# Two-layer encoder trunk on one core: gate, up and output projections in groups of six products, and a new order

## The chip, the core and the metric

The kernel runs on one core of a Trainium2 chip. The engines named below are TensorE (PE, matrix products; its weight loads are listed as PEld), VectorE (DVE), ScalarE (ACT), GpSimd (POOL) and SyncE (SP, which here issues the DMA transfers of the weights). The metric is the device time of one execution in microseconds (us), as the median of several runs; lower is better.

## The reference

The program computes two layers on one sequence of 256 rows of width 1024, all in float32. Cut to what matters here:

```python
def swiglu(x, w_gate, w_up, w_down):
    return (jax.nn.silu(x @ w_gate) * (x @ w_up)) @ w_down

def reference(x, mem, ...):
    mem_kv = mem @ w_mem_kv
    mem_k = split_heads(mem_kv[..., :MEM_WIDTH])
    mem_v = split_heads(mem_kv[..., MEM_WIDTH:])
    for i in range(DEPTH):                       # 2 layers
        x = layer_norm(ALPHA * x + 0.5 * swiglu(x, ffn1_w_gate[i], ffn1_w_up[i], ffn1_w_down[i]), ...)
        if i % N_MIXERS == 0:
            proj = x @ rwkv_w_in[j]              # 1024 -> 2560 + 256
            mix = rwkv7_mix(proj[..., :RWKV_SHIFT], ...)
        else:
            proj = x @ sb_w_in[j]                # 1024 -> 3*768 + 256
            mix = stick_breaking_mix(proj[..., :c], proj[..., c:2 * c], proj[..., 2 * c:3 * c])
        heads = jnp.concatenate([mix, memory_attention(mq, mem_k, mem_v)], axis=-1)
        x = layer_norm(ALPHA * x + heads @ w_out[i], ...)
        x = layer_norm(ALPHA * x + 0.5 * swiglu(x, ffn2_w_gate[i], ffn2_w_up[i], ffn2_w_down[i]), ...)
    return x
```

`rwkv7_mix` carries a 64 x 64 state for each of 12 heads along the 256 rows. `w_gate` and `w_up` are 1024 x 2816, `w_down` is 2816 x 1024. Most of the work is products of `x` with weights that are read once from memory.

## The kernel before

**Products in two parts.** PE multiplies a reduced float32 type (F32R) faster than float32, so most products are made of three. `piece()` loads 128 x 1024 weights into a raw buffer by DMA, ACT copies them to F32R (the high part, `hi`), and DVE subtracts that from the raw weights (the low part, `lo`). The rows of `x` are transposed on PE and split in the same way into `xTh` and `xTl`. `mm3` then adds, in one PSUM bank, xTh·hi, xTh·lo and xTl·hi. There are 11 raw, 9 high and 8 low buffers, which is why the same names (hi_7r, lo_8r) come again and again. In a matmul row of the profile `ps_29r<-hi_7r,xTh` reads: into bank ps_29r, hi_7r streams through (512 columns), and xTh is the stationary operand, 128 x 128.

**Tiles and stages.** The rows are two halves of 128. A feed-forward block (`ffn_block`) takes 256 columns of gate and of up: four pieces, each holding two of the eight 128-row steps k for 256 gate and 256 up columns. For each half 8 x 3 products go to a gate/up bank (ps_29r or ps_30r), then ACT and DVE make silu(gate)·up, PE transposes it, and `down` multiplies it into two accumulating banks of the half (ps_25r and ps_26r, ps_27r and ps_3r). For some blocks the down products are plain float32 ones, such as `ps_26r<-raw_51r,hT_945r`. Projections into the mixers and the output projection go through `cols_mm`, eight k with one `mm3` each. The transposes use banks ps_5r and ps_6r, which the mixers' small products use as well.

**What sets the order.** The code above doesn't issue anything: a planner (`Plan`) notes each operation with what it waits for, and a list scheduler then orders PE, DVE, ACT and the DMA queue of SP together, by a priority for each operation. The priorities stand in `URGENCY`, a packed table with one number for each operation in the order of the code. What `together()` encloses is one operation to the planner, an `mm3` for instance. The whole program is then issued in that order from one line in `Plan.issue` (L788 here, L785 in the changed kernel), so all rows of the profile show the same line, and groups are told apart by the names of the tiles.

**Stages in time.** From the start to 264 us the feed-forward blocks of the first layer run, then the mixer of the first half of the rows, whose state chain runs from 264 to 285 us. The state chain of the second half runs from 400 to 432 us. In such a chain products of the state (names with S_113r), additions on DVE, copies on ACT and products with L_345r follow each other for each chunk of 64 rows, and feed-forward products and projections fill PE between them. From 432 us on the feed-forward blocks of layer one and the whole of layer two follow, whose mixer has no such chain.

Of the kernel before, what the change touches and what calls it, by code (L numbers as in the profile page):

```python
# [18 lines left out]
AF = mybir.ActivationFunctionType  # L19
# [4 lines left out]
P = 128  # L24
D = 1024
KT = D // P
# [3 lines left out]
C = 64  # L30
# [7 lines left out]
FC = 256  # L38
# [34 lines left out]
FLAGS = dict(t1=False, bt=False, dc=False, out1=False, zl2=False, pb=False, xt=False, mn=False, tn=False, vn=False, sq=True)  # L73
# [45 lines left out]
class Engine_:  # L119
# [19 lines left out]
    'c-l?edAN<`8#exXZJ`Vel1617LVQJ~5}C>rqRb-7EK`I`Wr$LSMCK;Slp#|pG*IS>qJdB(A{9}r`}cX?{X35L{bL_{ueF}%zOVbb&g(qSYpq4?jW'  # L139
    'PDf62iEPL-_e@jPIvHSo{C~{J($qcFn#JLh3|}ef)hUX9#8d9-k4y$_p{h^!Sv=2mgw3_^}wryJv5%%-7$#D1<A#cI@}e=R02(LTk^hKJ|YexAJ('  # L140
    '!ADNH4U!M7Ru6rij9>V^`F-|xd<Fp1Lj6D)#hXXM_lr@Bh{VcG4`-?Jvf0NtwKg77r8kc4dp`|k|@N=KXH;A!a-VmBS6~d$r{>~S|oA&)j+%N8pv'
    '2TG8YJVH!(>FWh!59nrIb9)ye|N>$rd$Xmt^M)t7|WFop{cmCxc-49neiUa7DA14F>XGW`8b!yd;W{Dte9@I+{>QZw<v_JBSYx9C>=Ky3*q@ELMZ'
    'xFjJvCZutUD;&h+|(7{7G3`}V|m>D3`DbJj9qc=_WPH{KdT!8~&4JZI$bdgr-PEzbWE<42uBSo3#`n^wk{z9NKS_N*7x#C2a^A41JCav`>5kB9Jk'
    '+ZY#j58=v>V*I{r2%is%@tbQy7@-!goQW}iC9yi^DCd8%d<fS%%T3nVF2)sp3RDlFlCxc2G=z(<3L$ri5OVg7@f~qiliM4fjxn29N)-wr|H&A0T6'
    'e`maxIS!Hwodn4QjbQ#z&tCVaAuP^ZZn2*f%+ZLXXDy+vpIAf2Iz8w@~+D;;1Nw=-RPzxaF-F8~+sJyy+nfNQw8|7!URg;W0T~>8uxOsntX3Cy%+'
    'lk8y;!a@BF})9_R}#yQW&c%+8&zYXhm!%poG%J+zIbgvLPu2=f)F~0Cvj9+~i<6o^pxLfUOIM4TEVyq^A1=RA3>q59r9_wA33I!I*iSxX4PYA^d+'
    'wbmFsO{cdex8G+*{5SXaf@DZO`!+Hup-7iax?FS5WdV2W6|9q{AKN1+J}(6jI-FIhd#J5BO?@8k~`e>>YwrM3aPNOcskBcrT<SK6nid&()wc4Jux'
    'ml7Q)}lVti21n>B|MxNqc4kHX8579lLZS^n#VFkNj6sl`s`IaAHKPNd^2rBmVXzj8iMzF@lL+8B4~rTZI(Q2ogeIt+{PX8<mx*1y~z<LhnU4^FRX'
    'DZcz6xGc1mkN<v)u|%5~v&iuSS=2mxD*UQncER@eIWbO3$5_krH%<wm@_f1d2WA(9(0>TLT5}8>9~uzCp*Lb2G&qET{oNz>#baaKB7dtEIm2IK7#'
    '`zn*Z*)+jO*rwaI@!MUn3s5p3)rN9<g^<^{%d7W98nujel0#M!0C2{#CO9^1fBR#;t{!zti#D+i(Z7<3EqF^cx|dfcS&6uDw1LhMZ5w?)v>hn6Kb'  # L150
    '$-S?;COn90zTTN%B!tEE*@mGCx6Py-Q-%?+OFcGfmi=&FT#<UKhOScfF>Vt7JV;m`;ch?MIkep?mV$W;TXj2Fe&VtGPF}{qS3c~YfoHSgWs=g-wZ'
    '^7Ro_u_=Yui{>Lx+QBWZ2u!2d+Mvn_<NP}UDFQ+#6L;Sc2y1GQ#F6OMU3l<!@70vJC%-CKB}h9-&;R*EdhJhDsTV7xbS6!aqK(seGtM-N%&;4T09'
    'oQ{K_FL?4n0&$JnBGD&$`i;|#qr?|n7;i8lO|j`v(CrVsSXeXcDSLR<B?AcpdAGZQCGfd8w+T0^h2uN%Vme$Ny0P3~>|JFKZu3D<1KJ0Gjx2bZVg'
    'A9}OGarin8BOR^PEQE5MV;nNqHH}lDuo{-b7ro&ji#{DQFdh5;7D5v>p3y%Q=H3-!Q*q^8mX6zZ(WZ7G%!2O{a<TIzJmlV_*SpY^=k(meUfT&zv-'
    ';sPI=Esr9MFemU#Vxy5T2?Z!dcj@lkmR&>@mZ>8F&j%O~ogm61zLsr}}aVT)q7b{N)H?Bd+|g2_C+HSMlU1{Cz@gf2TS3;MF}-L%4jN`oewDYhr9'
    'Gwtg^QOOM<RFB|uzW1~G8Ve|*-SXYnFnPgwQw@IJg>h-E>)T>pDZ^`42@X=^pjQ{*Egs*Y)KxZu@)^_T(N*&(&I>!G-dAuitcm7Mq9l28B**v&Q4'
    '^&pGtn{bTelbr>$BcL6`{NMqxWrnkLwL7wI<8o(xBf>9^!A>LFh`Hp*|WQTObwUwg7S-tf02_s;wubOEk^Jat7v^T{joX5;>&R;JpU<<ulm3vt^b'
    '*3w<-xEH|d{RF^-XwT&rkIkq}PPuKn-DxWQ|CXw52|T8Iw4qNh&E?>2o=QS6r_7}C4V9uV*07)$#5o-bnTrj~nQex|%1_IEM$UaF?^)b>{W*HUfD'
# [633 lines left out]
def kernel(ctx, tc, const, x, mem, f1g, f1u, f1d, f2g, f2u, f2d, ln_g, ln_b, w_out, w_mem_kv,  # L792
                      rw_in, r_mu, r_w0, r_wup, r_a0, r_aup, r_gup, r_kk, r_ka, r_rk, r_lng, r_lnb, sb_in, out):
    nc = Plan(tc.nc)
# [206 lines left out]
    def ffn_block(w, c, halves, beside, whole):  # L1001
# [57 lines left out]
        hs = {}  # L1059
# [867 lines left out]
```

## Time and profile before

| | |
|---|---|
| Runs, median of 3 | 1056.89 us (1056.53 to 1056.94) |
| Profiled execution, own time | 1058.2 us |
| Its span in the profile | 1056.4 us, mean granted PE clock 0.995 |
| PE busy, PE weight loads busy | 99%, 79% of the span |
| DVE, ACT, POOL busy | 84%, 70%, 0% |
| DMA | 303.19 MB, 286 GB/s from and to HBM over the span |

The span is what the profiler recorded from the first to the last instruction; the own time of that execution has 1.8 us more around it, and is 1.3 us above the median of the runs. A busy share is an average over stages with different limits, so what counts is where PE waits. In the lists of groups and in the timelines the text in brackets, or after the last bar, is the idle time just before the instruction on its engine, and the engine and tile that ended it.

### The profile page before, as it was taken

What the parts mean: (1) busy time and instruction counts of PE and PEld (TensorE: products, weight loads), DVE (VectorE), ACT (ScalarE), POOL (GpSimd) and SP (SyncE); (2) the same over time, 40 slices, a digit from 0 to 9 for tenths busy, and PEclk for the clock granted to TensorE, in tenths of its full rate; (3) what the DMA queues carried; (4) which work ended last, traced back from release to release, by engine and by line L of the source; (5) the groups of instructions that cost most, each with busy time, mean ns of one, the idle gap of its engine ahead of it and who ended that gap; (6) DMA issues with size and microseconds to landing.
All of it is one profiled execution on the core that took longest, in us unless ns stands there. A gap on an engine that the chain in (4) does not pass through costs nothing.

```text
span 1056.4 us, 17846 instructions
## 1 busy us (share of the span) xinstructions
PE 1041.8 (99%) x6275; PEld 835.8 (79%) x6275; DVE 886.2 (84%) x1241; ACT 741.6 (70%) x1064; POOL 5.3 (0%) x20
## 2 busy tenths in 40 slices
PE   8999999999899999999999999999999999999997
PEld 7788888877788776688888888888778777888885
DVE  6776679999799998898799765569899999976688
ACT  6665558968679877667577555457987998765573
POOL 0000000000000000000000000000000000000000
PEclk9999999999899999999999999999999999999999
DMA  9998869879399788799999976768989989998792
GB/s 307 332 368 259 265 201 357 266 247 331 130 328 336 250 273 295 247 341 315 307 325 352 311 246 208 226 213 262 369 309 315 366 274 304 366 366 256 265 317 76
DMA packets 212684, 303.19 MB, mean 287 GB/s; under 512 B 13892, under 2 KB 159728, under 8 KB 212594
## 3 DMA queue, kind: packets, MB, share of 16 engines
q1 hardware_dynamic: 212050, 301.53, 85.2%
q8 instruction: 49, 0.80, 0.3%
q10 hardware_dynamic: 544, 0.52, 0.2%
q14 instruction: 41, 0.34, 0.1%
HBM read 300.95 MB, written 1.05 MB: 286 GB/s over the span
## 4 chain that ended last, share of the span: by engine, by line
PE 95%; DMA 2%; DVE 1%; ACT 1%; issue 0%; SPq 0%; DVEq 0%; ACTq 0%
PE ps_30r L788 28%; PE ps_29r L788 27%; PE ps_26r L788 8%; PE ps_3r L788 8%; PE ps_27r L788 8%; PE ps_25r L788 8%; PE ps_5r L788 3%; PE ps_6r L788 3%; DMA raw_9r<-in_ffn_w_down_dram 1%; DMA raw_18r<-in_ffn_w_up_dram 1%; DMA raw_48r<-in_ffn_w_up_dram 1%; DMA raw_12r<-in_ffn_w_up_dram 1%; DVE x L788 0%; DVE L_345r L788 0%; DVE lo_47r L788 0%
## 5 line engine op out<-in xcount | busy, mean ns | idle before, releaser
L788 PE MATMUL ps_30r<-hi_46r,xTh 128*128 128x512 f32 (+1 forms) x70 | 28.2, 403 | 0.0
L788 PE MATMUL ps_30r<-hi_46r,xTl 128*128 128x512 f32 (+1 forms) x70 | 26.9, 385 | 0.0
L788 PE MATMUL ps_30r<-lo_17r,xTh 128*128 128x512 f32 x68 | 26.5, 390 | 0.0
L788 PE MATMUL ps_29r<-lo_11r,xTh 128*128 128x512 f32 (+1 forms) x64 | 24.6, 385 | 0.8 <-DVE lo_11r L788 0.8
L788 PE MATMUL ps_30r<-lo_11r,xTh 128*128 128x512 f32 x64 | 25.0, 390 | 0.0
L788 PE MATMUL ps_30r<-hi_10r,xTh 128*128 128x512 f32 x60 | 24.5, 409 | 0.0
L788 PE MATMUL ps_30r<-lo_8r,xTh 128*128 128x512 f32 x62 | 24.2, 391 | 0.0
L788 PE MATMUL ps_30r<-hi_10r,xTl 128*128 128x512 f32 x60 | 23.5, 392 | 0.0
L788 PE MATMUL ps_30r<-lo_14r,xTh 128*128 128x512 f32 x60 | 23.4, 390 | 0.0
L788 PE MATMUL ps_29r<-hi_65r,xTh 128*128 128x512 f32 x56 | 22.8, 407 | 0.0
L788 PE MATMUL ps_29r<-lo_17r,xTh 128*128 128x512 f32 x58 | 22.6, 390 | 0.0
L788 PE MATMUL ps_29r<-lo_47r,xTh 128*128 128x512 f32 (+1 forms) x58 | 22.2, 383 | 0.0
L788 ACT ACTIVATE idle_2r<-ps_29r 128x256 f32<-128x256 f32 (+1 forms) x27 | 11.1, 412 | 15.8 <-PE ps_29r L788 15.2
L788 PE MATMUL ps_30r<-hi_7r,xTh 128*128 128x512 f32 (+1 forms) x56 | 21.9, 392 | 0.0
L788 PE MATMUL ps_29r<-hi_65r,xTl 128*128 128x512 f32 x56 | 21.9, 392 | 0.0
L788 ACT ACT_TABLE_LOAD x16 | 20.5, 1283 | 2.0 <-issue 1.7
L788 PE MATMUL ps_30r<-lo_41r,xTh 128*128 128x512 f32 x56 | 21.9, 390 | 0.0
L788 PE MATMUL ps_29r<-lo_14r,xTh 128*128 128x512 f32 x56 | 21.8, 390 | 0.0
L788 ACT ACTIVATE idle_1r<-ps_29r 128x256 f32<-128x256 f32 (+1 forms) x27 | 11.7, 432 | 14.3 <-PE ps_29r L788 14.3
L788 PE MATMUL ps_30r<-hi_7r,xTl 128*128 128x512 f32 (+1 forms) x56 | 21.4, 383 | 0.0
L788 PE MATMUL ps_30r<-hi_65r,xTh 128*128 128x512 f32 x52 | 21.4, 412 | 0.0
L788 ACT ACTIVATE idle_2r<-ps_30r 128x256 f32<-128x256 f32 (+1 forms) x30 | 12.9, 431 | 12.0 <-PE ps_30r L788 12.0
(2124 smaller groups left out, 3945.5 us busy)
## 6 DMA issues: line engine op xcount, KB each, us to landing
raw_9r<-in_ffn_w_down_dram SPq DMA_DIRECT2D x16, 512.0 KB, 6.7
raw_48r<-in_ffn_w_down_dram SPq DMA_DIRECT2D x16, 512.0 KB, 6.0
raw_12r<-in_ffn_w_down_dram SPq DMA_DIRECT2D x16, 512.0 KB, 6.2
raw_18r<-in_ffn_w_gate_dram SPq DMA_DIRECT2D x31, 256.0 KB, 5.0
raw_18r<-in_ffn_w_up_dram SPq DMA_DIRECT2D x31, 256.0 KB, 4.6
raw_15r<-in_ffn_w_down_dram SPq DMA_DIRECT2D x15, 512.0 KB, 5.8
raw_9r<-in_ffn_w_gate_dram SPq DMA_DIRECT2D x30, 256.0 KB, 5.9
raw_9r<-in_ffn_w_up_dram SPq DMA_DIRECT2D x30, 256.0 KB, 5.8
```

What stands on the lines that cost most here:

```text
L788: fn(*[at(x) for x in a], **{n: at(x) for n, x in k.items()})
```

## The change

In all gate and up products and in all projections through `cols_mm`, the eight steps k are taken in pairs. For the two k of a pair, `mm6` first makes the four products with the high part (xTh·hi and xTl·hi of the first k, then of the second), as one operation to the planner, and then the two products with the low part (xTh·lo of each), as a second operation. Before, each k had its own `mm3`: high, low, high. The products are the same, 5261 matmuls of the same shapes and operands; 944 triples become 472 groups of six. The down products and the products of the memory tokens keep `mm3`. Since two operations replace two, the table `URGENCY` keeps its length, and all its values are new, so that the order of the whole program is another one.

```diff
-FLAGS = dict(t1=False, bt=False, dc=False, out1=False, zl2=False, pb=False, xt=False, mn=False, tn=False, vn=False, sq=True)
+FLAGS = dict(t1=False, bt=False, dc=False, out1=False, zl2=False, pb=False, xt=False, mn=False, tn=False, vn=False, sq=True, lw=True)
...
 URGENCY = (
...
 )
...
+    def mm6(o, rows, start, stop):
+        with nc.together():
+            for i, (sh, sl, wh, wl) in enumerate(rows):
+                nc.tensor.matmul(o, sh, wh, start=start and i == 0, stop=False)
+                nc.tensor.matmul(o, sl, wh, start=False, stop=False)
+        with nc.together():
+            for i, (sh, sl, wh, wl) in enumerate(rows):
+                nc.tensor.matmul(o, sh, wl, start=False, stop=stop and i == len(rows) - 1)
+
     def cols_mm(o, xT, pieces):
+        if FLAGS["lw"]:
+            for i in range(0, KT, 2):
+                mm6(o, [(xT[0][:, k], xT[1][:, k], h, l) for k, h, l in pieces[i:i + 2]], i == 0, i == KT - 2)
+                yield
+                yield
+            return
         for i, (k, h, l) in enumerate(pieces):
             mm3(o, xT[0][:, k], xT[1][:, k], h, l, i == 0, i == KT - 1)
             yield
...
             if xs[group[0]] is None:
                 load_x(group[0])
-            for k in range(KT):
+            six = FLAGS["lw"] or FLAGS["l1"] and len(apart) > 1
+            for g in range(KT // 2) if six else ():
+                for hf in group:
+                    mm6(o[hf], [(xT[hf][0][:, 2 * g + j], xT[hf][1][:, 2 * g + j], gu[g][0][:, j], gu[g][1][:, j]) for j in range(2)],
+                        g == 0, g == KT // 2 - 1)
+                yield
+                yield
+            for k in () if six else range(KT):
                 wh, wl = (t[:, k % 2] for t in gu[k // 2])
                 for hf in group:
                     mm3(o[hf], xT[hf][0][:, k], xT[hf][1][:, k], wh, wl, k == 0, k == KT - 1)
```

Three places show how this moves instructions on PE. The first is the start of the program, from the second half of the first weight piece on (hi_7r with lo_8r); hi_10r with lo_11r and hi_13r with lo_14r are the next two pieces, and x_79 is the second half of the rows, which PE transposes. Rows that only repeat are left out. Before:

```order
L788 MATMUL ps_29r<-hi_7r,xTh 128x512
L788 MATMUL ps_29r<-lo_8r,xTh 128x512
L788 MATMUL ps_29r<-hi_7r,xTl 128x512
L788 MATMUL ps_29r<-hi_10r,xTh 128x512
L788 MATMUL ps_29r<-lo_11r,xTh 128x512
L788 MATMUL ps_29r<-hi_10r,xTl 128x512
L788 MATMUL ps_5r<-cst,x_79 128x128 x4
L788 MATMUL ps_29r<-hi_13r,xTh 128x512
L788 MATMUL ps_29r<-lo_14r,xTh 128x512
L788 MATMUL ps_29r<-hi_13r,xTl 128x512
```

The same place in the changed kernel:

```order
L785 MATMUL ps_29r<-hi_7r,xTh 128x512
L785 MATMUL ps_29r<-hi_7r,xTl 128x512
L785 MATMUL ps_29r<-lo_8r,xTh 128x512 x2
L785 MATMUL ps_29r<-hi_10r,xTh 128x512
L785 MATMUL ps_29r<-hi_10r,xTl 128x512
L785 MATMUL ps_29r<-lo_11r,xTh 128x512 x2
L785 MATMUL ps_29r<-hi_13r,xTh 128x512
L785 MATMUL ps_29r<-hi_13r,xTl 128x512
L785 MATMUL ps_29r<-lo_14r,xTh 128x512 x2
L785 MATMUL ps_5r<-cst,x_79 128x128 x4
L785 MATMUL ps_29r<-hi_16r,xTh 128x512
```

The low part of a piece is now read after four products with its high part instead of one, and the first transposes of x_79 stand behind three pieces instead of two (the second four behind four pieces instead of three).

The second place is the second state chain, on PE between the first products of the state (S_113r) and the first products with L_345r. Before:

```order
L788 MATMUL ps_6r<-S_113r,qr_377r 64x64 x2
L788 MATMUL ps_5r<-S_113r,qr_377r 64x64 x2
L788 MATMUL ps_26r<-raw_51r,hT_945r 128x512
L788 MATMUL ps_29r<-hi_49r,xTh 128x512
L788 MATMUL ps_29r<-lo_41r,xTh 128x512
L788 MATMUL ps_29r<-hi_49r,xTl 128x512
L788 MATMUL ps_5r<-L_345r,Tt_332r 64x64
L788 MATMUL ps_6r<-L_345r,Tt_332r 64x64
```

And in the changed kernel:

```order
L785 MATMUL ps_5r<-S_113r,qr_377r 64x64 x2
L785 MATMUL ps_6r<-S_113r,qr_377r 64x64 x2
L785 MATMUL ps_29r<-hi_7r,xTh 128x512
L785 MATMUL ps_29r<-hi_7r,xTl 128x512
L785 MATMUL ps_29r<-lo_23r,xTh 128x512 x2
L785 MATMUL ps_5r<-L_345r,Tt_332r 64x64
L785 MATMUL ps_6r<-L_345r,Tt_332r 64x64
```

Six projection products (two triples before, one group of six now) stand between S and L in both, and the float32 down product `ps_26r<-raw_51r,hT_945r` has left this place.

The third place is the same chain's next pass, on PE again. Before:

```order
L788 MATMUL ps_5r<-S_113r,qr_377r 64x64 x2
L788 MATMUL ps_6r<-S_113r,qr_377r 64x64 x2
L788 MATMUL ps_29r<-hi_13r,xTh 128x512
L788 MATMUL ps_29r<-lo_44r,xTh 128x512
L788 MATMUL ps_29r<-hi_13r,xTl 128x512
L788 MATMUL ps_29r<-hi_7r,xTh 128x512
L788 MATMUL ps_29r<-lo_50r,xTh 128x512
L788 MATMUL ps_29r<-hi_7r,xTl 128x512
L788 MATMUL ps_6r<-L_345r,Tt_332r 64x64
L788 MATMUL ps_5r<-L_345r,Tt_332r 64x64
```

And in the changed kernel:

```order
L785 MATMUL ps_6r<-S_113r,qr_377r 64x64 x2
L785 MATMUL ps_5r<-S_113r,qr_377r 64x64 x2
L785 MATMUL ps_25r<-raw_48r,hT_487r 128x512
L785 MATMUL ps_3r<-vn_314r,Sk_344r 64x64 x2
L785 MATMUL ps_27r<-vn_314r,Sk_344r 64x64 x2
L785 MATMUL ps_6r<-L_345r,Tt_332r 64x64
L785 MATMUL ps_5r<-L_345r,Tt_332r 64x64
```

Here a float32 down product and 24 small products of the chain itself (vn_314r, Sk_344r) have taken the place of the six projection products.

More of the change, by code (lines that the diff above doesn't have):

```diff
@@ new lines @@
+    '-g8|S&VxwT6=Abc`JtS{n;3Ior$rI^}Add!dCl#d?%kAQ|iwcE0hS~!u}ZZbPnO82{Haum_2Ve{>cz-VPEE{F`jwTUXRDvkqw78#n_ZzxkCsq)(W'
+    'AWxVG^+$E+A9H45QDu^j)656j0mzk3MPuM44;^%t@I#aSUdSHLkXW4uzlH$2RKYrf-e_b)LHE*Qcc|M4|*2oKrdKJmCIYX~dZ+BjDT@x~DT<#+RU'
+    'W2`+SgcFNmTqTy%uL@y^Sp2g!#-|?*;miTC=4*}1LYN>Y2j%pZd?EZOMq8$cO<BiV`_a-NG<_?^)Ap_Oa0tbB#kgr@jL$qECZ*Ww{9=5}++19{$2'
+    'e_LjBCaF>rNs3Q79ucn3;;pE)Su}ju>bC7ed}tDt<427n_Fg$#;DGFvj8MW9$h#xx0q2^RpO#X2<H^LnwGC6)$-tgp4sE%=dmK@orr?#!w@Kr})^'
+    '8AJtdKxCREMzYBBUr(!;9JU=kT@~~0<){HQ{QjC-Ti1A19J<ON6@>+k2wO@$wJUqVsGvC-dbEus3ko$W>DB-i8FNQGnrx^E-mN(e@_EOkA=dqexu'
@@ L291 @@
+    '`(2'
 )
```

295 lines of the change are left out of this document (143 added, 152 removed).

## The prediction

> **What bounds the kernel now.** I read the page first, for which engine is full and whether anything beside it is.
>
> ```profile
> span 1056.4 us, 17846 instructions
> PE 1041.8 (99%) x6275; PEld 835.8 (79%) x6275; DVE 886.2 (84%) x1241; ACT 741.6 (70%) x1064; POOL 5.3 (0%) x20
> ...
> PEclk9999999999899999999999999999999999999999
> DMA  9998869879399788799999976768989989998792
> ...
> PE 95%; DMA 2%; DVE 1%; ACT 1%; issue 0%; SPq 0%; DVEq 0%; ACTq 0%
> ...
> L788 ACT ACT_TABLE_LOAD x16 | 20.5, 1283 | 2.0 <-issue 1.7
> ```
>
> TensorE (PE) is busy for 99% of the span and makes up 95% of the chain that ended last. The change neither adds nor removes a product, so what can move is only the time in which PE waits, or works slowly. The view of stages says where that is (columns: length, then busy time of PE, its weight loads, DVE, ACT, POOL, then clock, DMA share, GB/s).
>
> ```profile
> 17.00:264.00 247.00, 246.80 (x1555) 199.23 (x1557) 203.52 (x292) 173.96 (x269) 1.20 (x3) 1.00 0.88 292
> 264.00:285.00 21.00, 17.82 (x386) 14.24 (x376) 15.68 (x37) 13.08 (x31) 1.40 (x4) 0.84 0.45 162
> 285.00:400.00 115.00, 114.97 (x778) 89.89 (x776) 111.26 (x193) 96.90 (x163) 0.95 (x2) 1.00 0.83 281
> 400.00:432.00 32.00, 31.40 (x611) 21.27 (x601) 25.68 (x35) 22.27 (x37) 0.26 (x1) 1.00 0.80 266
> 432.00:1048.50 616.50, 616.47 (x2914) 499.69 (x2913) 516.64 (x665) 425.25 (x552) 0.00 (x0) 1.00 0.88 294
> ```
>
> Outside the start and the two state chains of the first mixer (264 to 285 and 400 to 432 us) PE waits 0.20, 0.03 and 0.03 us. In the chains it waits 3.18 and 0.60 us. So before 1048.5 us there is little to win. The view of PE's waits names the releasers in the chains:
>
> ```profile
> PE ps_6r L788 <- DVE L_345r L788: 1.8, 2, 1.2
> PE ps_5r L788 <- DVE S_113r L788: 0.6, 1, 0.6
> PE ps_5r L788 <- ACT Lm_333r L788: 0.6, 1, 0.6
> PE ps_6r L788 <- ACT memKT L788: 0.5, 1, 0.5
> ```
>
> The third place is the start. This is its timeline (start, duration, engine, operation; in brackets the idle time before and who ended it):
>
> ```profile
> 7.41 0.69 DVE L788 TENSOR_TENSOR xTl<-ps_5r,xTh 128x512 fp32r<-128x512 f32 x1
> 8.15 0.50 PE L788 MATMUL ps_29r<-hi_7r,xTl 128*128 128x512 f32 x1 [0.19 <-DVE xTl L788]
> 9.29 0.50 PE L788 MATMUL ps_29r<-hi_10r,xTh 128*128 128x512 f32 x1
> 9.63 1.06 ACT L788 ACTIVATE hi_13r<-raw_15r 128x1024 fp32r<-128x1024 f32 x1 [0.39 <-DMA raw_15r<-in_ffn_w_up_dram]
> 10.55 0.50 PE L788 MATMUL ps_29r<-lo_11r,xTh 128*128 128x512 f32 x1 [0.76 <-DVE lo_11r L788]
> 10.71 1.23 DVE L788 TENSOR_TENSOR lo_14r<-raw_15r,hi_13r 128x1024 fp32r<-128x1024 f32 x1 [0.22 <-ACT hi_13r L788]
> 10.89 0.40 PE L788 MATMUL ps_29r<-hi_10r,xTl 128*128 128x512 f32 x1
> 11.19 1.06 ACT L788 ACTIVATE hi_16r<-raw_18r 128x1024 fp32r<-128x1024 f32 x1 [0.51 <-DMA raw_18r<-in_ffn_w_up_dram]
> 11.82 0.65 PE L788 MATMUL ps_5r<-cst,x 128*128 128x128 f32 x4
> 12.28 1.23 DVE L788 TENSOR_TENSOR lo_17r<-raw_18r,hi_16r 128x1024 fp32r<-128x1024 f32 x1 [0.34 <-ACT hi_16r L788]
> 12.54 0.39 PE L788 MATMUL ps_29r<-lo_14r,xTh 128*128 128x512 f32 x1
> 16.65 0.39 PE L788 MATMUL ps_29r<-hi_16r,xTl 128*128 128x512 f32 x1
> ```
>
> PE begins a product of hi_10r at 9.29, has lo_11r as the very next, and stands until 10.55: from start to start 1.26 us, where the next step (10.55 to 10.89) takes 0.34. That is 0.92 us lost to a low part that DVE had not finished. This is the wait at which the change acts.
>
> **The price of one product, and of the order itself.** Starts in the middle of the kernel:
>
> ```profile
> 306.17 0.39 PE L788 MATMUL ps_30r<-hi_43r,xTh 128*128 128x512 f32 x1
> 306.39 0.39 PE L788 MATMUL ps_30r<-lo_17r,xTh 128*128 128x512 f32 x1
> 306.62 0.39 PE L788 MATMUL ps_30r<-hi_43r,xTl 128*128 128x512 f32 x1
> ```
>
> A product takes 0.23 us from start to start (the 0.39 overlaps the next). From the first to the second the stationary operand (xTh) stays, from the second to the third it changes: 0.22 and 0.23. The page has as many weight loads as matmuls, 6275. So the reorder of the 944 triples into 472 groups of six costs 0 in itself. Its ends: below nothing only by waits, which come next; above, 944 kept operands lost, at 0.01 us each (the difference of the two steps) 9 us, which I don't take since that difference is the rounding of the starts. The Trainium skill (TensorE: Matmul & The Clock Gate, Part 2, step 1) says that weights are loaded apart so that one load can serve many matmuls; by that, giving up the shared operand would cost something. The trace does not agree for this program, which loads once per product anyhow.
>
> **The start, term by term.** With the new order (rows quoted with the change) PE has xTh for the first product at the old time and needs xTl for the second: 8.15, the end of the first DVE row above (7.41 + 0.69 = 8.10). From there, by 0.23 a product and 0.33 for the first after a wait: four products of hi_7r and two of lo_8r end at 9.40. hi_10r was in use at 9.29, so four products run to 10.32; lo_11r is there at 10.55 as before, its two products end at 11.12. hi_13r is ready at 9.63 + 1.06 = 10.69: four to 12.04, with lo_14r ready at 10.71 + 1.23 = 11.94, two to 12.50. Four transposes cost 0.49 (11.82 to 12.54, less one product). hi_16r is ready at 11.19 + 1.06 = 12.25: from 12.99 four to 13.91, lo_17r ready at 13.51, two to 14.37; four transposes to 14.86; the first piece for the other half, six products, to 16.24. The old order has just this work done at 16.65 + 0.23 = 16.88. The gain is **0.64 us**. Its ends: 0, if the next pieces don't come sooner and PE meets their DMA instead, and 0.92, the whole wait at lo_11r. I take 0.64, as every readiness on the way has a row. SP's first three DMAs are in another order (the constants now behind the first half row of x), but the first transposes need both, and the second ones the third DMA, which keeps its place: 0.
>
> **The second state chain, term by term.** Between the S products and the L products two adds on DVE and two copies on ACT must run; PE fills that time.
>
> ```profile
> 414.06 1.13 PE L788 MATMUL ps_26r<-raw_51r,hT_945r 128*128 128x512 f32 x2
> 416.50 0.27 PE L788 MATMUL ps_5r<-L_345r,Tt_332r 64*64 64x64 f32 x1
> 421.38 0.27 PE L788 MATMUL ps_5r<-S_113r,qr_377r 64*64 64x64 f32 x2
> 422.24 0.50 PE L788 MATMUL ps_29r<-hi_13r,xTh 128*128 128x512 f32 x1
> 424.47 0.27 PE L788 MATMUL ps_6r<-L_345r,Tt_332r 64*64 64x64 f32 x1 [0.57 <-DVE L_345r L788]
> ```
>
> The second time the fill is six products from 422.24, and L starts 2.23 us later, 0.57 of it waited. The first time a single-precision product stands ahead of the six, the fill is 2.44 us, and there is no wait. In the new order the first time has only the six: a new wait of 0.57. The second time has the single-precision product (2.44 less the six, 1.66, so about 0.8) and 24 small products (0.86, by S at 421.38 to 422.24): 1.66 of the 2.23, so 0.57 stays. Sum of the chain: **+0.57**. Ends: 0 (the adds, which run before one copy in one case and after both in the other, come out luckily) and +1.1 (both waits doubled). What queues behind the waiting L on PE is the next state update, so the wait is paid in full.
>
> **The first state chain.** From the gate products on, the new order has the same PE instructions with the same (few) projections between them; only two steps ahead of it change places. I take 0 of its 3.18 us; ends -3.18 and, if one of its releasers in the table above is late once more, +1.2.
>
> **The rest.** PE changes between projections and other work 335 times in the rows before and 355 times now, both ways counted, so there are ten more round trips. The first product after a break takes 0.34 (10.55 to 10.89) where 0.23 is usual: a trip costs between 0 and 0.10, ten of them 0 to +1.0. I take **+0.2**, near the lower end, since the 0.34 stands behind a stall and not behind other work. ACT has one table load more, 1.28 us (the last row of the page above); ACT is 70% busy, so it is covered, and if that cover is gone (a hi part late by 1.28, beside four products of 0.9 before its low part is wanted) PE would pay at most that once: ends 0 and +1.3, taken 0. The end of the kernel, from the last matmul on, has the same DVE instructions with two pairs exchanged: 0.
>
> Sum: -0.64 + 0.57 + 0.2 = +0.1 us. The profiled execution took 1058.2 us for a span of 1056.4, and the median of the runs is 1056.89; on the median this is **1057.0**. Differences under 0.2% (2.1 us) are about what a measurement of this kernel can tell from no change, so the forecast is no change to be told.
>
> **Rivals.**
> *The start's gain is eaten* (the change doesn't do what it does it for): DMA is at 90% or more in the first three slices of the page, so PE may wait for pieces instead of low parts. Then +0.8: 1057.7. Against it: after 10.55 the old order never waits for a DMA.
>
> *Faster, the chains close up.* The state chains wait 3.78 us together. If the new order's neighbours on DVE and ACT leave those engines free at the right time, 2.3 us or more of it go, with the start: 1054.5, at the most 1052.5. For it: these waits are decided by what stands ahead of the four releasers. Against it: the PE order there is nearly the same.
>
> *Slower, low parts come late between 285 and 400 us.* DVE is busy for 111.26 of 115 us there, 3.7 us of slack, and makes every low part (1.23 us by the rows above). Where two of them slip behind other DVE work PE waits 2.5 us and cannot win it back: 1059.5. It decides from the point where the slip is longer than the four products now put ahead, 0.9 us. Against it: exactly those products give each low part more time than before.
>
> *Slower, the clock gate.* Three rows of stages, cut at the edges of the slow clock:
>
> ```profile
> 271.27:274.69 3.42, 2.06 (x72) 1.53 (x70) 3.17 (x6) 1.88 (x6) 0.10 (x1) 1.00 0.23 87
> 274.69:278.10 3.41, 2.77 (x60) 2.25 (x58) 1.22 (x5) 3.05 (x9) 0.56 (x3) 0.50 0.02 5
> 421.45:424.86 3.41, 2.84 (x67) 2.16 (x68) 2.40 (x4) 2.33 (x4) 0.00 (x0) 1.00 0.71 218
> ```
>
> After a stretch with PE busy for 2.06 of 3.42 us the granted clock was 0.50. The stretch in the second chain had 2.84 and kept the clock. With the added wait it has some 2.3; should it lose the clock for two such stretches, half of 2 x 2.77 us of work is paid again, +2.8: 1059.8. The Trainium skill (TensorE: Matmul & The Clock Gate, Part 1) says that these windows run freely and are not reset by a kernel; by that, where an edge falls can differ between executions, and the same program could pay or not. The runs shown lie within 0.41 us of each other, so no run here shows it.
>
> *The kept operand counts after all*, the rule above: up to +9 us, 1066.
>
> **Chances.** Forecast 0.40; gain eaten 0.14; faster 0.20; late low parts 0.16; clock gate 0.08; kept operand 0.02. Faster by over 0.2%: 0.20. Within: 0.40 + 0.14 = 0.54. Slower: 0.26. The forecast's own range is 1055.5 to 1058.5, its ends being those of the terms without the first chain's. For 8 in 10 it must take in most of the faster case and the two slower ones: 1054.0 to 1059.8, which leaves out about 0.07 below and 0.11 above.
>
> **What would show it.** The start is right if the wait at lo_11r is some 0.2 us, and the two groups of transposes for the other half follow three and four pieces instead of two and three. The second chain is right if L waits twice. The order is free if products still start 0.23 us apart. I am wrong if PE's idle time between 285 and 400 or after 432 us is no longer under 0.1 us, if the slow clock shows outside 264 to 285, or if the first chain's 3.18 us change by more than 1.

## The result, and the profile after

The changed kernel took 1060.04 us (median of 7 runs, 1058.65 to 1062.41), the kernel before in the same comparison 1056.89 us (7 runs, 1056.23 to 1057.65). The ratio is 1.0029 (95% interval 1.0020 to 1.0038): slower by 3 us. The forecast was 1057.0, and its range ended at 1059.8.

The profiled execution of the changed kernel is its slowest run, 1062.41 us. The page:

```profile
span 1060.5 us, 17828 instructions
PE 1045.6 (99%) x6275; PEld 836.2 (79%) x6275; DVE 881.9 (83%) x1240; ACT 742.0 (70%) x1066; POOL 5.4 (1%) x20
...
PE 94%; DMA 3%; ACT 1%; DVE 1%; issue 0%; ACTq 0%; DVEq 0%; SPq 0%
```

The same 6275 matmul records keep PE busy for 1045.6 us instead of 1041.8, and the span is 4.1 us longer. So almost all of it is inside "busy" (1.4 us of it is one more stretch at half clock, as shown below). The view of stages says the same (columns as in the prediction):

```profile
17.00:264.00 247.00, 246.83 (x1532) 197.71 (x1531) 202.62 (x293) 172.33 (x264) 1.94 (x4) 1.00 0.88 289
264.00:285.00 21.00, 17.22 (x384) 13.51 (x382) 15.93 (x34) 13.87 (x31) 0.81 (x3) 0.79 0.55 191
285.00:400.00 115.00, 115.00 (x739) 90.85 (x738) 111.52 (x194) 97.92 (x163) 0.95 (x2) 0.99 0.84 278
400.00:432.00 32.00, 31.37 (x629) 20.93 (x631) 22.59 (x29) 23.44 (x38) 0.26 (x1) 1.00 0.82 276
432.00:1048.50 616.50, 616.47 (x2922) 497.33 (x2913) 513.86 (x665) 424.22 (x558) 0.00 (x0) 1.00 0.88 293
```

Outside the start and the two chains PE still waits for almost nothing: 0.17, 0.00 and 0.03 us where it was 0.20, 0.03 and 0.03. Only the granted clock of the first chain differs plainly, 0.79 where it was 0.84. PE's waits by releaser, the longest of them:

```profile
PE ps_5r L785 <- DVE L_345r L785: 1.7, 1, 1.7
PE ps_6r L785 <- ACT Lm_333r L785: 1.1, 2, 0.9
...
PE ps_29r L785 <- ACT xTh L785: 0.8, 1, 0.8
PE ps_6r L785 <- DVE S_113r L785: 0.7, 1, 0.7
```

The wait at lo_11r is gone, and a wait for xTh at the start has come. All of PE's idle time before its last product is 6.9 us, as against 6.7 (7.7 and 6.8 in a second profile of each kernel). To find the 4 us one has to look at something else than idle time: at the steps from the start of one product to the start of the next.

**Where the time went.** Up to the first product with S_113r in the first chain, PE does exactly the same work in both kernels, kind by kind (1785 matmul records, 948 of them projections; here and below that word stands for every product with a weight part, hi or lo), and from there to its last product it does the same again. So these two stretches can be compared. The table has them for two profiled executions of each kernel; the second ones are from the runs named before_again and after_again below. It is worked out from the starts of those products in the timelines.

| | before | before, again | changed | changed, again |
|---|---|---|---|---|
| first S product at | 271.52 | 270.96 | 272.35 | 272.24 |
| from there to the last product | 776.67 | 776.64 | 779.93 | 776.62 |
| slow windows of the clock in the first chain | 2 | 2 | 3 | 1 |
| from the first S product to the first projection after the chain | 12.10 | 12.10 | 13.50 | 11.23 |

A slow window is a stretch of 3.41 us with a granted clock of 0.50. The last row gives its price: 12.10 for two in either profile of before, 13.50 for three, 11.23 for one, so 1.40 and 0.87 us (new_consts_first, below, has none and takes 10.26). Put at two windows, the second row is 778.5 and 777.5 for the changed kernel. The change costs 1.1 us before the first chain and 0.9 to 1.9 us after it began, 2.0 to 3.0 us in all, and the number of slow windows comes on top by chance.

What these 2 to 3 us consist of can be read from all steps outside the first chain, sorted by what stands at their two ends:

| start to start, us lost | before | before, again | changed | changed, again |
|---|---|---|---|---|
| steps between projections, above 0.227 each (some 3370) | 3.3 | 2.9 | 4.6 | 4.1 |
| steps with other work at an end, against the first column | 0 | 0 | +1.5 | +0.8 |

The first row grows by 1.2 to 1.3 us, in small pieces. The second grows by 0.8 to 1.5 us; the second chain, whose small products are such steps, is in it.

Where in the program this happens can be read at points where PE has done the same number of products of each kind in all four profiles (us between two such points, named by the time at which the kernel before reaches them):

| stretch | before | before, again | changed | changed, again |
|---|---|---|---|---|
| 16.9 to 149.1 | 132.21 | 131.77 | 132.35 | 132.04 |
| 149.1 to 175.0 | 25.90 | 25.90 | 26.52 | 26.52 |
| 175.0 to 234.1 | 59.15 | 59.15 | 58.99 | 58.99 |
| 234.1 to 259.0 | 24.84 | 24.79 | 25.36 | 25.38 |
| 259.0 to 311.1, with the first chain | 52.08 | 52.12 | 53.96 | 51.42 |
| 311.1 to 388.0 | 76.95 | 76.91 | 76.80 | 76.94 |
| 388.0 to 452.0, with the second chain | 64.03 | 64.05 | 64.62 | 63.86 |
| 452.0 to 655.3 | 203.26 | 203.24 | 203.40 | 203.43 |
| 655.3 to 731.0 | 75.72 | 75.75 | 76.13 | 76.08 |
| 731.0 to 1047.0 | 315.97 | 315.92 | 316.36 | 316.25 |

Two short stretches, 149 to 175 and 234 to 259 us, hold 1.1 to 1.2 us of the loss, and they do so again in all four experiments below that keep the new order (26.54 to 26.86 and 25.37 to 25.51) and in neither of the two that keep the old one (25.96, and 24.81 to 24.96). The second chain loses 0.6 us in one pair and wins 0.2 in the other. In the first of these stretches PE takes a part of x as soon as DVE has made it, in the second a result of ACT. First two rows of the kernel before, then the changed one:

```profile
157.44 0.69 DVE L788 TENSOR_TENSOR xTl<-ps_5r,xTh 128x512 fp32r<-128x512 f32 x1
...
159.35 0.39 PE L788 MATMUL ps_29r<-hi_43r,xTl 128*128 128x512 f32 x1
```

```profile
156.66 0.68 DVE L785 TENSOR_TENSOR xTl<-ps_5r,xTh 128x512 fp32r<-128x512 f32 x1
...
157.01 0.48 PE L785 MATMUL ps_29r<-hi_40r,xTh 128*128 128x512 f32 x1
...
157.40 0.50 PE L785 MATMUL ps_29r<-hi_40r,xTl 128*128 128x512 f32 x1
...
157.73 0.39 PE L785 MATMUL ps_29r<-hi_40r,xTh 128*128 128x512 f32 x1
...
242.45 0.40 PE L785 MATMUL ps_3r<-hi_22r,hT_517r 128*128 128x512 f32 x1
242.52 0.36 ACT L785 ACTIVATE hT_487r<-ps_5r 128x256 f32<-128x256 f32 x1
...
242.94 1.13 PE L785 MATMUL ps_27r<-raw_9r,hT_487r 128*128 128x512 f32 x2
```

In the kernel before xTl is ready at 158.13 and PE first reads it 1.2 us later. In the changed one it is ready at 157.34 and read at 157.40; the two steps around that take 0.39 and 0.33 us, where 0.31 (the first stands behind transposes) and 0.23 are usual. At 242.94 hT_487r has been ready for 0.06 us, and the step before it takes 0.49 instead of 0.23. None of this is listed as idle time. With one more place in each stretch of the same kind (bank ps_30r at 160.42 and idle_1r at 241.74, ready 0.15 and 0.14 us before), these make up 0.4 of the 0.6 us that the first stretch loses and nearly all of the 0.5 of the second.

The smaller pieces look like this one of the changed kernel (timeline, columns as in the prediction):

```profile
594.44 1.06 ACT L785 ACTIVATE hi_13r<-raw_70r 128x1024 fp32r<-128x1024 f32 x1 [0.52 <-PE ps_29r L785]
...
595.37 0.39 PE L785 MATMUL ps_26r<-hi_7r,hT_1042r 128*128 128x512 f32 x1
...
595.60 0.46 PE L785 MATMUL ps_30r<-hi_13r,xTh 128*128 128x512 f32 x1
...
595.89 0.39 PE L785 MATMUL ps_30r<-hi_13r,xTl 128*128 128x512 f32 x1
...
596.12 0.40 PE L785 MATMUL ps_30r<-hi_13r,xTh 128*128 128x512 f32 x1
```

ACT has waited for PE to give the buffer hi_13r free, is done with the new high part at 595.50, and PE uses it at 595.60. The step from 595.60 to 595.89 takes 0.29 instead of 0.23, with no idle time in the record, since the modelled end of a product lies beyond the start of the next. The weight parts, too, have little reserve in the new order. I call reserve the time from the end of the operation that makes a weight part to the first product that reads it, and take all 510 high and 510 low parts after 17 us:

| parts with a reserve | before (both profiles) | changed (both profiles) | old order, sixes | new order, triples |
|---|---|---|---|---|
| high, under 1 us | 1, 0 | 36, 35 | 0 | 41 |
| high, under 0.3 us | 0, 0 | 8, 7 | 0 | 14 |
| low, under 0.3 us | 1, 0 | 8, 7 | 0 | 18 |

The last two columns are experiments, below. Most parts have as much reserve as before (the median of the high parts is 9.4 us before and 9.5 in the changed kernel). And the steps at weight parts with under 0.3 us make up only 0.3 to 0.5 us of the 1.2 to 1.3 in streams of projections. As much, 0.4 us, comes from four or five longer steps at 113, 157 to 160 and 286 us, where no weight part is that new; the rest is about 0.1 ns a step, and its cause is not known. ACT also meets the weights' DMA more often in the new order. Its waits for a DMA between 264 and 432 us, in the kernel before:

```profile
ACT hi_16r L788 <- DMA raw_70r<-in_w_out_dram: 1.3, 1, 1.3
```

and in the changed kernel, where there are ten with 8.3 us together (9.1 us in its second profile):

```profile
ACT hi_22r L785 <- DMA raw_18r<-in_rwkv_w_in_dram: 1.7, 1, 1.7
...
ACT hi_22r L785 <- DMA raw_64r<-in_w_out_dram: 1.2, 1, 1.2
```

Over the whole program after 17 us these waits come to 26 us in either profile of the changed kernel and to 12 and 17 in those of before. That they cost PE time is not shown: from 311 to 388 us, with two and four of them, it loses nothing.

The Trainium skill (Perfetto Trace Analysis, Identifying the Most-Contended Engine) says that the busy share of matmuls is not a good measure of how close a kernel is to its peak, because pipelined instructions look smaller in the trace. The trace agrees as far as it goes: the share is 99% in both kernels, and the busy time of the same matmuls differs by 3.8 us in the profiles shown and by 0.4 in the second ones.

### The profile page after: what moved, and what is told of

Same layout as the page of the kernel before. It is cut to its first block, busy times and chain, and to the rows that moved or that the text cites. A ratio compares the mean times of both kernels' runs of the same rounds, so it can differ in the third digit from the quotient of the medians.

```text
span 1060.5 us, 17828 instructions
## 1 busy us (share of the span) xinstructions
PE 1045.6 (99%) x6275; PEld 836.2 (79%) x6275; DVE 881.9 (83%) x1240; ACT 742.0 (70%) x1066; POOL 5.4 (1%) x20
## 4 chain that ended last, share of the span: by engine, by line
PE 94%; DMA 3%; ACT 1%; DVE 1%; issue 0%; ACTq 0%; DVEq 0%; SPq 0%
PE ps_30r L785 28%; PE ps_29r L785 28%; PE ps_27r L785 8%; PE ps_25r L785 8%; PE ps_26r L785 8%; PE ps_3r L785 8%; PE ps_6r L785 3%; PE ps_5r L785 3%; DMA raw_9r<-in_ffn_w_up_dram 1%; DMA raw_64r<-in_w_out_dram 1%; DMA raw_70r<-in_ffn_w_up_dram 1%; DMA x<-in_x_dram 0%; DVE x L785 0%; ACT Lm_333r L785 0%; ACT Y_340r L785 0%
## 5 line engine op out<-in xcount | busy, mean ns | idle before, releaser
L785 PE MATMUL ps_29r<-hi_22r,xTh 128*128 128x512 f32 x66 | 26.1, 395 | 0.0
L785 PE MATMUL ps_30r<-hi_16r,xTh 128*128 128x512 f32 x62 | 25.8, 417 | 0.0
L785 PE MATMUL ps_29r<-hi_22r,xTl 128*128 128x512 f32 x66 | 25.8, 391 | 0.0
L785 PE MATMUL ps_30r<-hi_13r,xTh 128*128 128x512 f32 x64 | 25.4, 398 | 0.0
L785 PE MATMUL ps_30r<-hi_13r,xTl 128*128 128x512 f32 x64 | 25.0, 390 | 0.0
L785 PE MATMUL ps_30r<-hi_16r,xTl 128*128 128x512 f32 x62 | 24.2, 391 | 0.0
L785 PE MATMUL ps_29r<-hi_7r,xTh 128*128 128x512 f32 x56 | 22.4, 400 | 0.8 <-ACT xTh L785 0.8
L785 PE MATMUL ps_29r<-hi_7r,xTl 128*128 128x512 f32 x56 | 22.0, 392 | 0.4 <-DVE xTl L785 0.4
L785 PE MATMUL ps_29r<-lo_47r,xTh 128*128 128x512 f32 x66 | 21.7, 410 | 0.0
L785 PE MATMUL ps_30r<-hi_7r,xTh 128*128 128x512 f32 x54 | 21.5, 399 | 0.0
```

What stands on the lines that cost most here:

```text
L785: fn(*[at(x) for x in a], **{n: at(x) for n, x in k.items()})
```

## The experiments

**Grouping and order apart.** The two tables are not exchanged. Instead the order is left as the planner makes it, and only when the two operations of a pair stand next to each other on PE are their six products issued in the other grouping:

```diff
+        for p, q in zip(pe, pe[1:]):
+            if p.i in self.pair and q.i == self.pair[p.i]:
+                six = p.calls + q.calls
...
+                six = [six[j] for j in (0, 2, 3, 5, 1, 4)]
...
+                six = [six[j] for j in (0, 4, 1, 2, 5, 3)]
```

The first list, two triples to four high and two low, makes old_order_sixes from the kernel before; the second, the way back, makes new_order_triples from the changed kernel. The start and stop marks of the sum are set anew in both.

> The old order of everything, but wherever the two triples of a pair stand next to each other on PE (343 of 472 pairs) the six products go out as four with the high part, then two with the low part. Theory 'order' (the grouping is free and the 3 us come with the new order): the wait at lo_11r goes, so 1056.0 us, 0.5 to 1.0 below the kernel before. Theory 'grouping' (a product costs more when its stationary operand is not kept): 343/472 of the 3.2 us, 1059.2 us, and the step from one product to the next is no longer 0.227 us.

Measured: 1057.78 us (11 runs) beside 1057.17 for the kernel before, ratio 1.000 (0.999 to 1.001). The grouping, here in 343 of the 472 pairs, costs nothing that can be told. The steps, at the place that the prediction showed for the kernel before:

```profile
306.44 0.39 PE L799 MATMUL ps_30r<-hi_43r,xTh 128*128 128x512 f32 x1
306.67 0.39 PE L799 MATMUL ps_30r<-hi_43r,xTl 128*128 128x512 f32 x1
306.90 0.62 PE L799 MATMUL ps_30r<-lo_17r,xTh 128*128 128x512 f32 x2
307.35 0.39 PE L799 MATMUL ps_30r<-hi_49r,xTh 128*128 128x512 f32 x1
```

From 306.44 to 307.35 are four steps of 0.23. But the gain at the start did not come either:

```profile
10.65 0.73 PE L799 MATMUL ps_29r<-lo_11r,xTh 128*128 128x512 f32 x2
11.93 0.66 PE L799 MATMUL ps_5r<-cst,x 128*128 128x128 f32 x4 [0.55 <-DMA x<-in_x_dram]
```

The wait at lo_11r is down to 0.07 us, and 1.3 us later PE waits 0.55 us for the DMA that brings the other half of x. That is the rival "the start's gain is eaten".

> The new order of everything, but wherever the two parts of a group stand next to each other on PE (284 of 472 groups) they go out as two triples high, low, high. Theory 'order': as slow as the changed kernel or a little slower, 1060 to 1061 us, with a wait of 0.9 us at lo_11r back at the start. Theory 'grouping': 284/472 of the loss is gone, 1058.1 us.

Measured: 1064.8 us (5 runs), ratio 1.0073 (1.0057 to 1.0088), some 5 us slower than the changed kernel. Both theories had it wrong: the new order needs the grouping. A triple asks for its first low part three products, 0.68 us, earlier than a group of six, and in the new order PE then reads 18 of these parts less than 0.3 us after they are made, some after a wait:

```profile
962.39 0.50 PE L796 MATMUL ps_29r<-lo_41r,xTh 128*128 128x512 f32 x1 [0.47 <-DVE lo_41r L796]
962.73 0.39 PE L796 MATMUL ps_29r<-hi_22r,xTl 128*128 128x512 f32 x1
```

So the grouping gives time, and the new order uses it up where low parts come late. That something was bought with it is not to be seen: in the old order nearly all low parts were there in time anyway.

**The clock.** Both kernels once more, unchanged, for the clock of each run:

> The kernel before, unchanged, for the granted clock of each of its runs. Theory 'clock' (the new order meets one slow window of 3.4 us more): the clock of its runs is higher by 0.0016 on the mean than that of the changed kernel's runs (0.9960), that is 0.9976, and runs of both kernels with the same clock differ by under 1 us. Otherwise the clocks agree and the runs differ by about 3 us at the same clock.

> The changed kernel, unchanged, beside the others on one chip: 1060 us by every theory; its runs spread by 1.7 us for each slow window of the clock more or fewer (0.0016 of mean clock) if the slow clock is paid in full.

Measured: 1057.47 us (12 runs, ratio 1.0005, 0.9996 to 1.0014) and 1059.45 us (11 runs, ratio 1.0025, 1.0013 to 1.0038). Over all runs of these two programs in this study the mean granted clock is 0.9958 (89 runs of before) and 0.9959 (18 of the changed kernel): the new order does not lose the clock more often. With the clock of a run its time moves, by 0.7 us for 0.001 in either kernel, and at the same clock the changed kernel is slower: 1061.17 and 1058.14 us at 0.995 (3 and 20 runs), 1059.11 and 1057.40 at 0.996 (4 and 35), 1058.48 and 1056.13 at 0.998 (4 and 2). A straight line through each puts them at 1058.3 and 1056.0 at 0.998, a difference of 2.3 us. So the rival "the clock gate" is not the cause of these 2.3 us. It explains why the profile shown had 4.1 us: there the slow clock lasted for three windows.

```profile
272.77:276.18 3.41, 1.42 (x60) 1.15 (x51) 3.06 (x8) 2.30 (x8) 0.33 (x2) 1.00 0.39 144
276.18:279.59 3.41, 2.79 (x71) 2.50 (x74) 0.75 (x4) 2.96 (x9) 0.47 (x2) 0.50 0.02 5
279.59:283.00 3.41, 2.76 (x48) 2.44 (x43) 2.96 (x9) 1.56 (x3) 0.00 (x0) 0.50 0.40 116
283.00:286.42 3.42, 3.42 (x24) 2.83 (x22) 2.17 (x10) 1.19 (x4) 0.00 (x0) 0.50 0.00 0
```

In the second profile of the same program it lasted for one, in new_consts_first it did not come. The Trainium skill (TensorE: Matmul & The Clock Gate, Part 1) says that the windows run freely and aren't set back when a kernel starts; by that one program can pay for a different number of them from run to run. These two profiles agree with it, where no run shown before the prediction could.

**The start.** The changed kernel's first product began at 8.01 us, that of before at 7.22. One thing undone, the order of SP's first DMAs:

```diff
+        loads = [j for j, (_, _, o) in enumerate(order) if o.eng == "SP"][:2]
+        assert self.pull(order, loads[1], loads[0])
```

`pull` takes the operation at the first place out of the order and puts it in at the second, if nothing in between stands against it.

> The changed kernel with one thing undone: SP issues the constants ahead of both row pieces of x again, as before the change. Theory 'head' (the row piece ahead of the constants delays the first weights on ACT's own queue, and with them xTh, so that the gain at the start is lost): PE begins the first product at 7.2 us instead of 8.0 to 8.2, and the time falls by 0.6 to 0.9 us, to 1058.8 us. Rival (the landing of those DMAs varies by itself): the first product begins anywhere between 7.2 and 8.2 with either order, and the time stays within 0.3 us of the changed kernel's.

Measured: 1059.51 us (12 runs), ratio to before 1.0021 (1.0011 to 1.0032). The first product began at 7.35, but the time stayed within what can be told from the changed kernel's. In the five profiles with the changed order of these DMAs the first product began at 7.29 to 8.19, in the five with the old one at 7.02 to 7.39. So the new order of the DMAs probably starts later more often than not, and the landing varies by 0.9 us within it; but the time does not follow. At the point that the kernel before reaches at 16.9 us new_consts_first was 0.8 to 0.9 us ahead of it, more than the forecast 0.64, and at 29 us by 0.1 at most. The start of the changed kernel, for comparison:

```profile
6.32 1.15 ACT L785 ACTIVATE hi_7r<-raw_9r 128x512 fp32r<-128x512 f32 x2 [3.09 <-DMA raw_9r<-in_ffn_w_up_dram]
8.01 0.49 PE L785 MATMUL ps_29r<-hi_7r,xTh 128*128 128x512 f32 x1 [0.83 <-ACT xTh L785]
11.11 0.62 PE L785 MATMUL ps_29r<-lo_11r,xTh 128*128 128x512 f32 x2
```

ACT gets the first weights at 6.32, copies them, and only then xTh; PE waits 0.83 us for that, and no longer at lo_11r.

Next, in the old order with groups of six, the two groups of transposes that had met the DMA go one weight piece later, as in the new order:

```diff
+        for turn, some in zip(turns, (mms[4:6], mms[8:10])):
+            for o in some:
+                assert self.pull(order, where(o), where(turn))
```

> The old order with groups of six, and at the start one thing more: the two groups of transposes of the other half go one weight piece later, as in the new order. Theory 'eaten' (in the old order the grouping took away the wait at lo_11r, 0.77 us, and PE then waited 0.55 us for the DMA of x at these transposes): no wait at either place, 0.5 us below the old order with groups of six, 1057.0 us, and 0.2 to 0.5 us below the kernel before. Rival: the wait moves on to the next piece, and nothing changes.

Measured: 1057.30 us (11 runs), ratio to before 0.9997 (0.9988 to 1.0005). Both waits are gone from its timeline, and 23 us later there is another, 0.43 us for lo_50r at 35.08, where the first profile of before has 0.20 and the second none. The rival was nearer: the wait moved on, though not to the next piece, and the time is not to be told from that of the kernel before. Until about 35 us what PE wins it waits for at the next place, in these profiles for a part whose weights came late. The clearest case is in the kernel mended below, which was 0.84 us ahead of the second profile of the changed kernel until 25 us:

```profile
25.38 0.71 PE L820 MATMUL ps_30r<-lo_11r,xTh 128*128 128x512 f32 x2
26.98 0.50 PE L820 MATMUL ps_29r<-hi_13r,xTh 128*128 128x512 f32 x1 [0.89 <-ACT hi_13r L820]
```

ACT waited 1.8 us for the DMA of raw_9r there, and the lead was gone at 27 us.

**Is it this order or the grouping?** Both kernels with an empty table, for which the planner makes 50 rounds of its own search, with two seeds:

```diff
-URGENCY = (
...
-)
+URGENCY = ""
-SEED = 53017
+SEED = 7
```

The seed is changed in the second pair only.

> Triples, and no table: the planner seeks an order for itself in 50 rounds. By itself it says how far an order found in this short way is behind the table's: some us by each theory. It is the partner of the next kernel.

> Groups of six, and no table: the planner seeks an order for itself in 50 rounds, from the same seed. Theory 'draw' (an order is one draw among many, and its small waits decide, not the grouping): the two differ by more than 2 us, in either direction. Theory 'grouping helps': with the longer time for each low part the planner finds an order that is faster by 1 us or more than the partner's. Theory 'grouping harms': slower by about 3 us.

> Triples, the planner's own 50 rounds, from another seed; the partner of the next. With the first seed it gave 1073.7 us.

> Groups of six, the planner's own 50 rounds, from that other seed. With the first seed it was 7.3 us faster than triples. Theory 'grouping helps the search': again faster than its partner by 2 us or more. Theory 'draw': the difference is under 2 us or of the other sign, and the seeds differ among themselves by as much as the two groupings.

Measured: with the first seed 1073.75 us for triples and 1066.40 for sixes (4 runs each; ratios to before 1.0153, 1.0136 to 1.0170, and 1.0089, 1.0072 to 1.0106), with the second 1069.92 and 1069.78 (1.0120, 1.0105 to 1.0134, and 1.0125, 1.0110 to 1.0141). The grouping gains 7 us or nothing, and one grouping differs by 3.4 to 3.8 us from seed to seed. So an order found in 50 rounds is a draw, and its scatter is larger than the 2.3 us in question; these orders are 9 to 16 us behind the tables' ones, and the scatter of those is not known. Two seeds don't tell whether the grouping helps a search on the mean. And reserve of the weight parts does not rank orders: in these four not one high part and at most three low ones have under 0.3 us, better than in the changed kernel, and they are slower.

**Mending the small waits.** In the changed kernel, at 18 places where a part's reserve was under 0.3 us or a step between projections was long, the next PE operation that depends on nothing in between goes ahead (it could at 16):

```diff
+        for o in late:
+            j = where(o)
+            for f in [f for f in range(j + 1, len(order)) if order[f][2].eng == "PE"][:4]:
+                if self.pull(order, f, j):
...
+                    break
```

> The changed kernel with 16 places mended: where a product with a weight part began less than 0.3 us after that part was made, or stood more than 18 ns too long behind another product, the next PE operation that depends on nothing in between goes ahead of it. Theory 'reserve' (the new order uses weight parts, the high ones above all, as soon as they are made, and PE pays a little at each): under ten parts with less than 0.3 us are left, and PE's steps inside streams of products lose 0.7 to 1.0 us less, so 1058.5 to 1059.0 us. Rival (these small waits are not lost time, or others take their place): the steps lose as much as before, and the time stays at 1059.5 us.

Measured: 1060.80 us (5 runs), ratio 1.0036 (1.0024 to 1.0049). The parts with under 0.3 us of reserve fell to 4, as meant. But operations that were taken ahead met waits of their own, 0.73 and 0.51 us from start to start at 664 and 958 us. A second version leaves those places alone and mends 10:

> The changed kernel with 10 places mended: those of the 16 whose move opened a wait at the place that it was taken from (five of them) are left as they were. Theory 'reserve': PE's steps inside streams of products lose 0.4 us less than in the changed kernel and no new wait opens, so 0.4 us below it, 1059.1 us. Rival (what is won at one place is lost at the next): those steps lose as much as in the changed kernel, within 0.1 us, and the time stays at 1059.5 us or above.

Measured: 1059.63 us (12 runs), ratio 1.0019 (1.0008 to 1.0031), not to be told from the changed kernel. After 452 us its steps between projections lose 1.6 us where the changed kernel's second profile has 2.1, the forecast 0.4; but all steps there together lose 13.9 us where it was 13.3. So each theory got half: the steps in streams lose less, as the first said, and the time stays, as the rival said, since more is lost where PE changes to other work. The small waits are where time is recorded, but it is not shown that taking them away brings it back. The two stretches at 149 and 234 us, where most is lost, are not shorter in either version (26.54 and 26.55, 25.51 and 25.40 us); no run takes the waits there away.

The profile of this last run (1065.28 us, its slowest) shows what little reserve can cost. ACT:

```profile
318.16 1.06 ACT L820 ACTIVATE hi_16r<-raw_18r 128x1024 fp32r<-128x1024 f32 x1 [1.98 <-DMA raw_18r<-in_ffn_w_up_dram]
319.57 1.06 ACT L820 ACTIVATE hi_10r<-raw_48r 128x1024 fp32r<-128x1024 f32 x1 [0.35 <-DMA raw_48r<-in_rwkv_w_in_dram]
320.65 1.28 ACT L820 ACT_TABLE_LOAD   x1
321.95 0.60 ACT L820 ACTIVATE Lm_333r<-ps_3r 128x512 f32<-128x512 f32 x1
```

PE, and the clock in the two windows after it and in the next:

```profile
322.60 0.49 PE L820 MATMUL ps_3r<-zl_315r,kn_313r 64*128 64x128 f32 x2 [1.10 <-ACT Lm_333r L820]
```

```profile
323.90:327.31 3.41, 3.41 (x15) 2.99 (x15) 1.95 (x4) 2.32 (x6) 0.00 (x0) 0.50 1.10 346
327.31:330.72 3.41, 3.41 (x14) 3.02 (x13) 2.11 (x4) 2.51 (x8) 0.00 (x0) 0.51 0.92 307
330.72:334.13 3.41, 3.41 (x21) 2.92 (x21) 3.41 (x7) 3.41 (x6) 0.00 (x0) 1.00 0.41 151
```

Two late DMAs, 2.3 us together, hold ACT; the copy for the mixer stands behind them and a table load; PE waits 1.1 us, and the clock is halved for two windows at a place where no other profile has it. In the profile of new_consts_first PE waited 0.5 us at the same place, in the other four of the new order none is listed, and in the four of the old order ACT waits for no weights at all between 300 and 340 us. This fits the wider spread of the changed kernel (its runs lie 1.2 us about the line through their clocks, those of before 0.6), though one such profile doesn't prove that it makes it.

## Why the prediction was wrong, step by step

- **What bounds the kernel.** "So before 1048.5 us there is little to win" was read as if there were also little to lose: outside the start and the two chains the sum has no term but the +0.2 for breaks, because PE's listed waits there are 0.20, 0.03 and 0.03 us. That is the step that failed. The listed waits stayed as small (0.17, 0.00 and 0.03), and 1.1 to 1.3 us were lost all the same between 17 and 259 us and 0.8 to 1.0 from 452 us to the end, in steps of 0.29 to 0.49 us instead of 0.23 that no idle time shows. The signs of being wrong were put on idle time too. Only the slow clock went past its sign, to 286.4 us instead of 285, in the profile shown.
- **The order of the six.** 0 in itself: right, by old_order_sixes. The rival of the kept operand (up to +9 us) is out.
- **The start.** The wait at lo_11r went, as forecast, and the transposes stand where they were expected. The sum of -0.64 did not come: at 17 us the changed kernel was ahead by 0.30 us in one profile and 0.04 in the other, since xTh came 0.8 us later, and at 29 us it was no longer ahead. "Every readiness on the way has a row" held for one execution; the landing of the DMAs varies by as much as the gain. The rival "the start's gain is eaten" was right about the start; "the old order never waits for a DMA" was true of PE, but in the rows shown ACT waits 0.51 us for one at 11.19.
- **The second state chain.** +0.57 did not come as worked out: L waits in neither pass, where the sign asked for two waits. PE's waits between 400 and 432 us are these two:

```profile
PE ps_27r L785 <- issue: 0.3, 1, 0.3
PE ps_6r L785 <- ACT Lm_333r L785: 0.2, 1, 0.2
```

  Together with two shorter ones 0.63 us, where it was 0.60. Six projections were enough in the first pass, with no wait (1.58 us from the first of them to L): the assumption that S to L takes as long as in the second pass before was false. That the stretch with this chain is 0.6 us longer in the profile shown is luck; in the second profile it is 0.2 shorter.
- **The first state chain.** 0 was right at an equal number of slow windows. With two of them the stretch from the first S product to the first projection after the chain takes 12.15 us in the new order (new_order_triples, new_order_mended_2) and 12.10 in the old.
- **The rest.** Ten more breaks came, as counted, but a break has no price of its own. Two, four and eight transposes between projections add 0.23, 0.45 and 0.88 us in all four profiles, and two and four records of float32 down products 0.87 and 1.73; going from one kind to the other and back adds 0.01 at most. From 731 to 806 us, through part of the second layer's mixer, both kernels take the same time within 0.02 us. What grew is the number of breaks at which PE stands: of those with transposes and float32 products alone, two before are over 0.06 us too long, 0.5 us together; now six or seven are, 1.1 to 1.3 us together, and at five of them an operand had been ready for only 0.05 to 0.15 us. So +0.2 was not a size to be corrected: it priced the wrong thing. ACT's further table load came (17); what it cost was not told apart.
- **Left out of the sum.** Operands that come just in time. By the trace these are parts of x, bank ps_30r, idle_1r and hT_487r in the two stretches that lose most, ready 0.05 to 0.15 us before PE needs them, and a few weight parts elsewhere. The rival "low parts come late between 285 and 400 us" was near it, but in one stage, which lost nothing, and on one engine. Among the weight parts more high ones than low ones lost their reserve (under 1 us: high 1 before and 36 now, low 64 and 73); for 14 of the 36 ACT had stood idle until PE gave the buffer free. That the missing reserve is the cause is read from the traces; no run restores it and wins the time back.
- **The clock gate.** As a price of the change: out. It moves single runs by 0.9 to 1.4 us a window.
- **Faster, the chains close up.** They did not: 3.18 us of waits in the first became 3.78.
- **The range.** "Its ends being those of the terms" does not come out: the ends named for the terms add up to -0.9 and +3.4, or 1056.0 and 1060.3, not 1055.5 and 1058.5. The added ends would have held the measured time, by luck, since none of those terms is what grew.

## What to carry to other kernels

A bound engine that never idles can still lose: compare its busy time for the same instructions, and its steps from start to start, before reading "no waits" as "nothing can happen". When a change gives an operand more time, see first whether anything was waiting for that operand, and then, in the new order of instructions, how much reserve all the other operands are left with, the activations as well as the weights. When two profiles hold the same work, compare the time between points of equal work: a loss that has no place in a list of waits has one there. An order found by a short search is a draw, and a gain of one known wait is small beside the scatter of such draws (here 0.6 us beside 3 to 7).

## What the runs showed of the hardware

- The same program paid for three slow windows of 3.41 us in one profile and for one in the other, in the same place (a kernel that differs in two DMAs had none); each costs 0.9 to 1.4 us there.
- A product that reads its operand 0.05 to 0.11 us after it was made can be late with no idle time in its record, and the step behind it is 0.06 to 0.11 us longer (0.29 to 0.34 instead of 0.227).
- Changing between projections, transposes and float32 products costs PE 0.01 us at most: 0.11 us for each transpose and 0.43 for each record of a float32 product, whether two or more stand together.
- The first product begins at 7.02 to 8.19 us in ten profiles; with one and the same order of the first DMAs it moves by up to 0.9 us from profile to profile.
